# Value projection of four recurrent heads in 512-column matmuls, and a shared ring of three, in a hybrid decoder layer

## The chip, the cores and the metric

The kernel runs on one core of one Trainium2 chip. The metric is device time in microseconds, the median of several executions. Beside it stands one execution taken by the hardware profiler, whose span and rows are quoted below. The engines are TensorE (PE for its matmuls, PEld for its weight loads), VectorE (DVE), ScalarE (ACT), GpSimd (POOL) and SyncE (SP), which issues most of the transfers.

## The reference

One decoder layer over 2048 positions of width 1024, all in float32. The input is normalised and projected. Four recurrent heads (key and value width 128) and eight attention heads with a window of 128 read the projection; their outputs are joined, projected and added to the input. A gated feed-forward part with a causal convolution of width three and a last normalisation follow. Cut to the lines that matter here:

```python
u = rmsnorm(h, norm_mix_w[l])
proj = u @ w_in[l]
hq, hf, hi, hg, att = jnp.split(proj, [...], axis=-1)
f = lb + (1.0 - lb) * jax.nn.sigmoid(hf)
k_hg = 1.0 - f
v_hg = hi.reshape(B, S, HG_HEADS, HG_DV)          # four heads of 128 columns
o_hg = hgrn2_chunkwise(q_hg, k_hg, v_hg, log_f)   # S_t = diag(f_t) S_{t-1} + k_t v_t^T, o_t = S_t^T q_t
o_hg = rmsnorm(o_hg, hg_norm_w[l]) * silu(hg)
...
h = h + mix @ w_out[l]
```

The change touches `hi @ w`, the value projection, and the products that the recurrence needs.

## The kernel before

The sequence is worked through in two halves of 1024 positions. Each half has a mixing part (attention and recurrent heads, then the output projection) and a feed-forward part. Activations lie transposed, channels on partitions.

**Precision.** Every large product is made of three matmuls in a reduced float32 format. An operand is split into `hi`, its rounded copy, and `lo`, the rest: `hi*hi + hi*lo + lo*hi`. For weights `prep` does it (lines L192 on ACT and L193 on DVE), from a raw tile that SyncE fetches into a ring of three ("raw", L184). The two results go into a ring of two ("hi", "lo"), or, with `slots`, into the eight slots with the tag "m" that also hold queries, gates and later results.

**A unit** (`unit`, L214) projects to 128 channels: eight contraction tiles, three matmuls each, for two banks of 512 positions, so 48 matmuls with 512 moving columns.

**The value projection** (`project_v`, L706 to L710) is the one that puts positions on partitions. The stationary operand is a 128x128 tile of the input, the moving one the weights. Before, it serves two heads at a time: for each of eight position tiles 24 matmuls with 256 moving columns, and then two ACT instructions (L710) that scale each head's 128 columns into the head's own tile. It is called in heads 0 and 2 of each half, after the query unit of the attention.

**A recurrent head** (`hgrn`) goes through stages, each ended by a `yield`: the units f and hq; then element products whose sums over channels are made on PE (`summed_products`: d on DVE, L546, hi on ACT, L547, lo on DVE, L548, two matmuls into `pdiag`, L550 and L551); then levels of 1, 2, 4, 8, 16, 32 and 64 positions. For each level beyond the first, ACT gathers parts of QK into a tile G (L598), PE multiplies them (`plev`, L604 and L609), and DVE multiplies QK by the decay (L612) and places the results into ST. Then come transposes (`pkn`), the state updates (`pu` and SS, L657), the gate unit g, the outputs (`po`, L671 and L672), a normalisation and last transposes (`pot`, L687). Banks of PSUM for `pdiag`, `plev`, `pkn`, `pu`, `po` and `pot` come from a pool of two.

**An attention pair** (`attend`) makes its query unit, scores (`psc`), softmax, transposes (`ppt`) and outputs (`poT`).

**Order.** The main loop steps the two generators alternately. A planner turns this order into one fixed queue per engine: an earlier instruction in the program has precedence, but a later one may overtake it when the earlier isn't ready. So PE runs units of the next head while a chain waits. In heads 0 and 2 the query unit and the value projection stand as follows, and head 3 makes its gate unit ahead of the levels:

```python
elif h % 2 == 0:
    next(at)
    wv = [prep(a["w_v"][h // 2, s]) for s in range(2)]
    next(hg)
    vs += project_v(hf, wv, X, rs, p)
else:
    next(hg)
    next(at)
```

The output projection (`out_proj`, matmuls `pop`) can start only when all units of the half are done, since its operands take over the input's tiles; its third unit is held behind marks of head 3 (`BEHIND`).

Of the kernel before, what the change touches and what calls it, by code (L numbers as in the profile page):

```python
# [8 lines left out]
F32 = mybir.dt.float32  # L9
F32R = mybir.dt.float32r  # L10
U32 = mybir.dt.uint32
I32 = mybir.dt.int32
AF = mybir.ActivationFunctionType
# [4 lines left out]
P = 128  # L18
D = 1024
KT = D // P  # L20
# [3 lines left out]
TT = HALF // P  # L24
NB = HALF // 512
HG = 4
# [13 lines left out]
NEG = -1.0e30  # L40
UT = 7
RAW = 3
VB = 2
GB = 2
WARM = 12
TAIL_WARM = 7
LV = 4
# [3 lines left out]
def hymba_layer(ctx: ExitStack, tc: tile.TileContext, a: dict, out: bass.AP):  # L51
    nc = tc.nc

    def pool(name, bufs=1, space=None, stack=ctx, **kw):
        if space is not None:
            kw["space"] = space
        return stack.enter_context(tc.tile_pool(name=name, bufs=bufs, **kw))
# [12 lines left out]
    def ps(kind, name):  # L70
        return spaces[kind].tile([P, 512], F32, tag=kind, name=name)
# [109 lines left out]
    def raw4(src):  # L181
        t = wp.tile([P, D], F32, tag="raw", name="raw", bufs=RAW)
        if src is not None:
            nc.sync.dma_start(t, src)  # L184
        return t

    def prep(src, slots=False):

        raw = raw4(src)
        hi, lo = [hp.tile([P, D], F32R, tag="m", name=f"w{t}", bufs=KT) if slots else  # L190
                  wp.tile([P, D], F32R, tag=t, name=f"w{t}", bufs=2) for t in ("hi", "lo")]
        nc.scalar.copy(hi, raw)  # L192
        nc.vector.tensor_tensor(lo, raw, hi.bitcast(F32), op=ALU.subtract)  # L193
        return hi, lo
# [327 lines left out]
    def hgrn(hf, h, X, invb, vs, WG, mix, p, fu=None):  # L522
# [18 lines left out]
        ST = p.tile([P, TT, P], F32, tag="t4", name="ST", bufs=2)  # L541
        def summed_products(x, y):

            d = p.tile([P, 512], F32, tag="dd", name="dd", bufs=2)
            hi, lo = [p.tile([P, 512], F32R, tag="dg", name=n, bufs=4) for n in ("dh", "dl")]
            nc.vector.tensor_tensor(d, x, y, op=ALU.mult)  # L546
            nc.scalar.copy(hi, d)  # L547
            nc.vector.tensor_tensor(lo, d, hi.bitcast(F32), op=ALU.subtract)  # L548
            o = ps("hg", "pdiag")
            nc.tensor.matmul(o, ones_r, hi, start=True, stop=False)  # L550
            marks[1] = nc.tensor.matmul(o, ones_r, lo, start=False, stop=True)  # L551
            return o
# [35 lines left out]
        for m in LEVELS:  # L588
# [7 lines left out]
            if m > 1:  # L596
                G = p.tile([P, 2, HALF // 2], F32, tag="G", name="G", bufs=GB)
                nc.scalar.copy(G.rearrange("p t (b c m) -> p t b c m", c=2, m=m), far)  # L598
                pl = ps("hg", "plev")
                if m == 32:  # L600
                    for c in range(TT):
                        for b in range(2):
                            x = slice(c % R * P + b * 64 + c // R * m, c % R * P + b * 64 + c // R * m + m)
                            nc.tensor.matmul(pl[2 * b * m:2 * b * m + m, c * m:(c + 1) * m], G[:, 1, x], G[:, 0, x],  # L604
                                             start=True, stop=True)
# [33 lines left out]
        v = vs[h]  # L639

        Kn = p.tile([P, TT, P], F32, tag="t4", name="Kn", bufs=2)
        for b in range(NB):
            pk = ps("hg", "pkn")
            for i in range(4):
                c = slice((b * 4 + i) * P, (b * 4 + i + 1) * P)
# [3 lines left out]
        for b in range(NB):  # L649
            pu = ps("hg", "pu")  # L650
            for i in range(4):
                c = 4 * b + i
                marks["pu"] = nc.tensor.matmul(pu[:, i * P:(i + 1) * P], Kn[:, c], v[:, c], start=True, stop=True)
            for i in range(4):
                c = 4 * b + i
# [11 lines left out]
        for c in range(TT):  # L667
            cs = slice(c * P, (c + 1) * P)
            prev = state[:, h] if c == 0 else SS[:, c - 1]
            o = po[c // 4][:, c % 4 * P:(c % 4 + 1) * P]  # L670
# [5 lines left out]
        rs = rsqrt(ss, TT, 1.0 / P)  # L676
# [7 lines left out]
        for b, bs in halves():  # L684
# [4 lines left out]
            if h == HG - 1:  # L689
                hi, lo = mix[h]  # L690
# [4 lines left out]

    def project_v(hf, parts, X, rs, p):

        v = [p.tile([P, TT, P], F32, tag="v", name="v", bufs=VB) for _ in range(2)]
        for tt in range(TT):
            o = ps("mm", "pvv")  # L700
            t = slice(tt * P, (tt + 1) * P)
            for kt in range(KT):
                hi, lo = parts[kt // 4]
                xh, xl = X[kt]
                c = slice((kt % 4) * 256, (kt % 4 + 1) * 256)
                nc.tensor.matmul(o[:, 0:256], xh[:, t], hi[:, c], start=kt == 0, stop=False)  # L706
                nc.tensor.matmul(o[:, 0:256], xl[:, t], hi[:, c], start=False, stop=False)
                nc.tensor.matmul(o[:, 0:256], xh[:, t], lo[:, c], start=False, stop=kt == KT - 1)
            for i in range(2):
                nc.scalar.activation(v[i][:, tt], o[:, i * P:(i + 1) * P], AF.Identity, scale=rs[:, tt:tt + 1])  # L710
        return v

    def split_into(h, l, src, eng=None):
        return (nc.scalar.copy(h, src),  # L714
# [480 lines left out]
    for hf in range(NH):  # L1195
        X, kv, invb, rs, f0 = nxt
        with ExitStack() as st:
            p = pool(f"mix{hf}", stack=st, reuse_waits="tile")
            KS, V = att_keys(hf, kv, invb, p)
            mix = [None] * KT  # L1200
            vs = []
            M, WG = {}, {}
            for h in range(HG):
                hg = hgrn(hf, h, X, invb, vs, WG, mix, p, f0 if h == 0 else None)
                at = attend(hf, h, X, invb, KS, V, mix, p)
                with tc.issue_after(summed.ins) if hf + h == 0 else ExitStack():
                    next(hg)
                if h == HG - 1:
                    next(at)
                    next(hg)  # L1210
                    for kt in (0, 4, 1, 5, 2, 6):
                        M[kt] = split(mix[kt])
                    next(hg)
                elif h % 2 == 0:
                    next(at)
                    wv = [prep(a["w_v"][h // 2, s]) for s in range(2)]
                    next(hg)
                    vs += project_v(hf, wv, X, rs, p)
                else:
                    next(hg)  # L1220
                    next(at)
                if h < HG - 1:
                    WG[h] = prep(a["w_g"][h])
                next(at)
                next(hg)
                if h < HG - 1:
                    next(hg)
                next(at)
                if h < HG - 1:
# [5 lines that stand above are left out]
            M[7], M[3] = mix[7], mix[3]  # L1235
        with ExitStack() as st:
            p = pool(f"ffn{hf}", stack=st, reuse_waits="tile")
            kept, ops, hs, first, last = out_proj(hf, M, p)
            acts = gate_up(hf, ops, hs, first, last, p)
            nxt = down(hf, kept, acts, p)  # L1240


def _layout(i):

    import numpy as np

    def cols(w, idx):
        t = w[:, idx].reshape(KT, P, len(idx))
        return t.transpose(1, 0, 2).reshape(P, -1)

    x = i["x"][0]
    w_in = i["w_in"][0]
    ar = np.arange
    att0 = 2048
    att = [np.concatenate([att0 + j * HD + ar(HD), att0 + (j + 4) * HD + ar(HD)]) for j in range(4)]
    att += [att0 + 512 + ar(P), att0 + 640 + ar(P)]
    b = i["b_attn"][0]
    rows = [ar(P) + h * P for h in range(4)]
    rows += [512 + np.concatenate([j * HD + ar(HD), (j + 4) * HD + ar(HD)]) for j in range(4)]
    w_out = i["w_out"][0][np.concatenate(rows)]  # L1260
    w_v = np.stack([cols(w_in, 1024 + pr * 256 + ar(256)).reshape(P, 2, D).transpose(1, 0, 2) for pr in range(2)])
    conv = np.concatenate([i["conv_w"][0], i["conv_b"]], 0)
    d = {
        "xT": x.T.reshape(KT, P, S),
        "norm_mix_w": i["norm_mix_w"][0].reshape(KT, P).T,
        "w_q": np.stack([cols(w_in, h * P + ar(P)) for h in range(4)]),
        "w_f": np.stack([cols(w_in, 512 + h * P + ar(P)) for h in range(4)]),
        "w_v": w_v,
        "w_g": np.stack([cols(w_in, 1536 + h * P + ar(P)) for h in range(4)]),
        "w_att": np.stack([cols(w_in, c) for c in att]),  # L1270
        "b_attn": np.stack([b[c - att0] for c in att], 1),
        "lb_logits": i["lb_logits"].reshape(2, HG, P).transpose(2, 0, 1),
        "hg_norm_w": i["hg_norm_w"].reshape(P, 1),
        "sinks": i["sinks"].reshape(2, 4).T.reshape(1, 8),
        "w_out": np.stack([cols(w_out, t * P + ar(P)) for t in range(KT)]),
        "norm_ffn_w": i["norm_ffn_w"].reshape(KT, P).T,
        "final_norm_w": i["final_norm_w"].reshape(KT, P).T,
        "w_gate": np.stack([cols(i["w_gate"][0], t * P + ar(P)) for t in range(FT)]),
        "w_up": np.stack([cols(i["w_up"][0], t * P + ar(P)) for t in range(FT)]),
        "conv": conv.reshape(4, FT, P).transpose(2, 1, 0),  # L1280
    }

    w = i["w_down"][0].reshape(FT // 2, 2, P, 2, 4, P)
    d["w_down"] = w.transpose(3, 1, 2, 0, 4, 5).reshape(4, P, FT // 2, 512)
    return {k: np.ascontiguousarray(v) for k, v in d.items()}
# [16 lines left out]
```

## Time and profile before

| | |
|---|---|
| median of three executions | 2175.64 us (2173.93 to 2177.19) |
| the profiled execution | 2174.83 us, its span 2173.1 us |
| mean granted TensorE clock | 0.999 |
| PE / PEld busy | 99% / 83% of the span |
| DVE / ACT busy | 76% / 50% |
| mean share of the DMA engines | 119 GB/s moved |

Busy time is the union of the instructions' intervals. Matmuls are pipelined and overlap, so PE's busy share says that it is never idle for long, not that each matmul needs its duration. Rows of instruction groups give line, engine, operation, what it writes and reads, partitions and elements, count, and then busy us, mean ns of one, and the idle time before. Rows of the timeline give start and duration in us.

### The profile page before, as it was taken

The page shows a single profiled execution, that of the slowest core. Times are in us where ns is not written, and L with a number is a line of the kernel's source. Part 1 is how long each engine was busy: PE and PEld are TensorE (multiplying, and loading weights), DVE is VectorE, ACT ScalarE, POOL GpSimd, SP SyncE. Part 2 cuts the span into 40 slices and gives each one's busy share as a digit, 9 for nine tenths or more (in the row PEclk, how much of TensorE's full clock was granted, in tenths as well). Part 3 has the DMA queues.
Part 4 walks back from the last instruction along what each step waited for, and adds up shares of the span by engine and source line. Part 5 has one row for each costly group of instructions (what it writes and reads, how often), then busy time and mean ns, then how long its engine had stood idle before and what let it go on. Part 6 is the DMA issues. An engine that isn't in the chain of part 4 may idle for free.

```text
span 2173.1 us, 29038 instructions
## 1 busy us (share of the span) xinstructions
PE 2151.3 (99%) x11136; PEld 1809.6 (83%) x11136; DVE 1659.9 (76%) x2446; ACT 1094.1 (50%) x1902; POOL 6.0 (0%) x28
## 2 busy tenths in 40 slices
PE   9999999999999999999999999999999999999998
PEld 7988987888888888788889889878888888888888
DVE  6677677688887878785866776777978888887766
ACT  6556556564444445335736466555544443444353
POOL 1000000000000000000000000000000000000000
PEclk9999999999999999999999999999999999999999
DMA  4101112413232235964631111124133323259643
GB/s 156 49 30 39 49 40 78 136 59 127 92 126 89 96 117 167 375 223 163 205 127 39 42 37 49 47 70 147 58 116 102 117 82 126 93 190 396 226 142 131
DMA packets 94387, 258.09 MB, mean 119 GB/s; under 512 B 11416, under 2 KB 17576, under 8 KB 94248
## 3 DMA queue, kind: packets, MB, share of 16 engines
q1 hardware_dynamic: 88992, 251.30, 34.2%
q10 hardware_dynamic: 5256, 4.94, 0.8%
q8 instruction: 87, 1.43, 0.3%
q14 instruction: 52, 0.43, 0.1%
HBM read 195.10 MB, written 57.15 MB: 116 GB/s over the span
## 4 chain that ended last, share of the span: by engine, by line
PE 93%; DVE 3%; ACT 2%; DMA 1%; issue 1%; SPq 0%; ACTq 0%; DVEq 0%
PE X L885 7%; PE pop L214 7%; PE X L887 7%; PE X L886 7%; PE hq L214 4%; PE f L214 4%; PE q L214 4%; PE g L214 4%; PE Y L885 4%; PE Y L886 4%; PE Y L887 4%; PE pdx L1098 3%; PE pdx L1096 3%; PE pdx L1097 3%; PE pdy L1096 3%; PE pdy L1097 3%
## 5 line engine op out<-in xcount | busy, mean ns | idle before, releaser
L714 ACT CAST whi<-raw 128x1024 fp32r<-128x1024 f32 x88 | 92.6, 1052 | 109.1 <-PE X L886 68.2
L885 PE MATMUL X<-T,whi 128*128 128x512 f32 x352 | 136.9, 389 | 0.0
L886 PE MATMUL X<-T,whi 128*128 128x512 f32 x352 | 136.9, 389 | 0.0
L887 PE MATMUL X<-T,wlo 128*128 128x512 f32 x352 | 136.9, 389 | 0.0
L980 DVE SCALAR_TENSOR_TENSOR y<-ga,cw,y 128x1024 f32<-128x1024 f32 x88 | 112.4, 1280 | 26.0 <-ACT y L978 26.0
L892 ACT COPY u<-X 128x512 f32<-128x512 f32 x88 | 51.5, 585 | 133.2 <-PE X L887 133.0
L715 DVE TENSOR_TENSOR wlo<-raw,whi 128x1024 fp32r<-128x1024 f32 x88 | 107.2, 1219 | 0.0
L715 DVE TENSOR_TENSOR xld<-raw,xhd 128x1024 fp32r<-128x1024 f32 x72 | 80.9, 1132 | 21.7 <-ACT xhd L714 21.2
L192 ACT CAST whi<-raw 128x1024 fp32r<-128x1024 f32 x57 | 59.9, 1050 | 72.2 <-PE pop L214 28.6
L714 ACT CAST xhd<-raw 128x1024 fp32r<-128x1024 f32 x72 | 69.6, 977 | 47.3 <-DMA raw<-act1T 15.5
L193 DVE TENSOR_TENSOR wlo<-raw,whi 128x1024 fp32r<-128x1024 f32 x57 | 69.2, 1217 | 26.4 <-ACT whi L192 26.3
L214 PE MATMUL pop<-XH,wlo 128*128 128x512 f32 x256 | 85.9, 390 | 0.0
L214 PE MATMUL pop<-XL,whi 128*128 128x512 f32 x256 | 85.2, 390 | 0.0
L214 PE MATMUL pop<-XH,whi 128*128 128x512 f32 x256 | 85.0, 393 | 0.0
L886 PEld LDWEIGHTS X<-T,whi 128*128 128x128 f32 x352 | 66.1, 188 | 13.8
L885 PEld LDWEIGHTS X<-T,whi 128*128 128x128 f32 x352 | 66.1, 188 | 13.7
L887 PEld LDWEIGHTS X<-T,wlo 128*128 128x128 f32 x352 | 66.1, 188 | 13.7
L1096 PE MATMUL pdx<-xhd,hid 128*128 128x512 f32 x192 | 74.5, 392 | 1.9 <-ACT hid L714 1.0
L1097 PE MATMUL pdx<-xld,hid 128*128 128x512 f32 x192 | 74.8, 390 | 0.0
L612 DVE TENSOR_TENSOR QK<-QK,f 128x1024 f32<-128x1024 f32 x56 | 68.5, 1223 | 8.2 <-ACT G L598 7.6
L1098 PE MATMUL pdx<-xhd,lod 128*128 128x512 f32 x192 | 73.7, 389 | 0.0
L706 PE MATMUL pvv<-whi,XH 128*128 128x256 f32 x256 | 72.7, 286 | 0.0
(384 smaller groups left out, 6601.1 us busy)
## 6 DMA issues: line engine op xcount, KB each, us to landing
wr<-in_w_down SPq DMA_DIRECT2D x90, 512.0 KB, 5.5
raw<-in_w_gate SPq DMA_DIRECT2D x44, 512.0 KB, 3.7
raw<-in_w_up SPq DMA_DIRECT2D x44, 512.0 KB, 3.7
raw<-act0T SPq DMA_DIRECT2D x20, 512.0 KB, 3.9
raw<-act1T SPq DMA_DIRECT2D x20, 512.0 KB, 5.7
act0B<-y SPq DMA_DIRECT2D x33, 256.0 KB, 2.2
act1B<-y SPq DMA_DIRECT2D x33, 256.0 KB, 2.8
raw<-in_w_out SPq DMA_DIRECT2D x16, 512.0 KB, 6.2
```

The source lines that it names most:

```text
L193: nc.vector.tensor_tensor(lo, raw, hi.bitcast(F32), op=ALU.subtract)
L214: marks["unit"] = nc.tensor.matmul(o[b], w, x[:, bs], start=f, stop=l)
L706: nc.tensor.matmul(o[:, 0:256], xh[:, t], hi[:, c], start=kt == 0, stop=False)
L714: return (nc.scalar.copy(h, src), (eng or nc.vector).tensor_tensor(l, src, h.bitcast(F32), op=ALU.subtract))
L715: (eng or nc.vector).tensor_tensor(l, src, h.bitcast(F32), op=ALU.subtract))
L885: nc.tensor.matmul(o, wh[:, ws], xh, start=i == 0 and not more, stop=False, skip_group_check=more)
L886: nc.tensor.matmul(o, wh[:, ws], xl, start=False, stop=False, skip_group_check=more)
L887: r = nc.tensor.matmul(o, wl[:, ws], xh, start=False, stop=i == 3, skip_group_check=more)
L980: nc.vector.scalar_tensor_tensor(y, g[:, w:w + HALF], C.cw[:, ft, w:w + 1], y, op0=ALU.mult, op1=ALU.add)
L1096: nc.tensor.matmul(o, wh[:, i, c], ah[:, i, cols], start=f, stop=False, skip_group_check=more)
L1097: nc.tensor.matmul(o, wh[:, i, c], al[:, i, cols], start=False, stop=False, skip_group_check=more)
L1098: nc.tensor.matmul(o, wl[:, i, c], ah[:, i, cols], start=False, stop=l, skip_group_check=more)
```

## The change

`project_v` is called once in each half, in head 0, for all four heads: its matmuls have 512 moving columns, one ACT instruction evacuates all four heads of a position tile, and the values lie in one tile for four heads. The value weights are laid out in four tiles of two contraction tiles each; the first two are split into the ring of two, the last two into "m" slots. Head 2 now takes the same order of steps as head 1. In `summed_products` the tiles "dd" (two of 512) and "dg" (four of 512) are gone; d takes one slot and the pair hi, lo another slot of the ring "G" of the gathered copies, whose slots hold 2 x 512 and whose number goes from two to three.

```diff
-VB = 2
-GB = 2
+GB = 3
...
-            d = p.tile([P, 512], F32, tag="dd", name="dd", bufs=2)
-            hi, lo = [p.tile([P, 512], F32R, tag="dg", name=n, bufs=4) for n in ("dh", "dl")]
+            d = p.tile([P, 2, 512], F32, tag="G", name="dd", bufs=GB)[:, 0]
+            both = p.tile([P, 2, 512], F32R, tag="G", name="dh", bufs=GB)
+            hi, lo = both[:, 0], both[:, 1]
...
     def project_v(hf, parts, X, rs, p):
 
-        v = [p.tile([P, TT, P], F32, tag="v", name="v", bufs=VB) for _ in range(2)]
+        v = p.tile([P, HG, TT, P], F32, name="v")
         for tt in range(TT):
             o = ps("mm", "pvv")
             t = slice(tt * P, (tt + 1) * P)
             for kt in range(KT):
-                hi, lo = parts[kt // 4]
+                hi, lo = parts[kt // 2]
                 xh, xl = X[kt]
-                c = slice((kt % 4) * 256, (kt % 4 + 1) * 256)
-                nc.tensor.matmul(o[:, 0:256], xh[:, t], hi[:, c], start=kt == 0, stop=False)
-                nc.tensor.matmul(o[:, 0:256], xl[:, t], hi[:, c], start=False, stop=False)
-                nc.tensor.matmul(o[:, 0:256], xh[:, t], lo[:, c], start=False, stop=kt == KT - 1)
-            for i in range(2):
-                nc.scalar.activation(v[i][:, tt], o[:, i * P:(i + 1) * P], AF.Identity, scale=rs[:, tt:tt + 1])
-        return v
+                c = slice((kt % 2) * 512, (kt % 2 + 1) * 512)
+                nc.tensor.matmul(o, xh[:, t], hi[:, c], start=kt == 0, stop=False)
+                nc.tensor.matmul(o, xl[:, t], hi[:, c], start=False, stop=False)
+                nc.tensor.matmul(o, xh[:, t], lo[:, c], start=False, stop=kt == KT - 1)
+            nc.scalar.activation(v[:, :, tt], o.rearrange("p (h d) -> p h d", h=HG), AF.Identity,
+                                 scale=rs[:, tt:tt + 1])
+        return [v[:, h] for h in range(HG)]
...
-                elif h % 2 == 0:
+                elif h == 0:
                     next(at)
-                    wv = [prep(a["w_v"][h // 2, s]) for s in range(2)]
+                    wv = [prep(a["w_v"][s], s > 1) for s in range(4)]
                     next(hg)
                     vs += project_v(hf, wv, X, rs, p)
...
-    w_v = np.stack([cols(w_in, 1024 + pr * 256 + ar(256)).reshape(P, 2, D).transpose(1, 0, 2) for pr in range(2)])
+    w_v = cols(w_in, 1024 + ar(512)).reshape(P, 4, D).transpose(1, 0, 2)
```

The tiles take the same room: per partition 8 KB for two value tiles, 8 KB for G, 4 KB for dd and 8 KB for dg before; 16 KB and 12 KB after.

## The prediction

> **What bounds the kernel now.** I read the page's first part, then the waits of TensorE (PE), then the busy time by stage of the first half of the sequence.
>
> ```profile
> span 2173.1 us, 29038 instructions
> PE 2151.3 (99%) x11136; PEld 1809.6 (83%) x11136; DVE 1659.9 (76%) x2446; ACT 1094.1 (50%) x1902; POOL 6.0 (0%) x28
> ...
> PE poT L508 <- DVE pp L500: 3.5, 5, 1.5
> PE pu L653 <- ACT Kn L647: 2.5, 2, 1.4
> ```
>
> PE is the bound, nearly everywhere; its largest waits (us in total, times, longest) come where the last recurrent head of a half ends. Columns of the next view: stretch and length, then busy us and instructions of PE, PEld, DVE, ACT, POOL, then clock and DMA.
>
> ```profile
> 69.11:97.80 28.69, 28.69 (x267) 28.41 (x266) 16.39 (x27) 18.33 (x37) 0.00 (x0) 1.00 0.12 37
> ...
> 155.20:234.40 79.20, 79.20 (x517) 68.21 (x516) 64.85 (x119) 51.53 (x115) 0.00 (x0) 1.00 0.14 40
> ...
> 307.90:352.77 44.87, 44.87 (x259) 38.07 (x258) 42.98 (x63) 31.28 (x48) 0.00 (x0) 1.00 0.39 117
> ...
> 353.00:380.00 27.00, 23.32 (x185) 19.80 (x184) 17.32 (x46) 13.01 (x58) 0.00 (x0) 1.00 0.01 2
> 1430.90:1457.90 27.00, 23.42 (x186) 19.79 (x185) 17.03 (x44) 13.07 (x58) 0.00 (x0) 1.00 0.01 2
> ```
>
> The five stretches are: value projection of head 0; head 1; head 3 up to the end of its levels; the rest of head 3; and that same rest in the second half. PE is full in the first three. DVE is idle 12.3 us beside the projection (28.69 - 16.39), but takes 82% of head 1 (64.85 of 79.20) and 96% of head 3's first stretch (42.98 of 44.87). In the rest of head 3 PE idles 3.7 us (27.00 - 23.32), 3.6 us in the second half: there the chain of head 3 is late and PE has nothing else. So PE work removed is worth its full time only while the recurrent chains keep up with the shorter queue.
>
> **The matmuls.** The duration of a matmul is not its price, because they overlap; the distance of starts is. First and last row of 11 projection matmuls in a row, and of 12 with 512 moving columns that also change their weights each time:
>
> ```profile
> 78.33 0.28 PE L706 MATMUL pvv<-whi,XH 128*128 128x256 f32 x1
> ...
> 79.53 0.28 PE L707 MATMUL pvv<-whi,XL 128*128 128x256 f32 x1
> ...
> 504.10 0.39 PE L885 MATMUL X<-T,whi 128*128 128x512 f32 x1
> ...
> 506.60 0.39 PE L887 MATMUL X<-T,wlo 128*128 128x512 f32 x1
> ```
>
> 256 columns: 1.20 / 10 = 0.120 us. 512 columns: 2.50 / 11 = 0.227 us. Each of three lines (L706 to L708) runs 256 times, 768 in all; they become 384 of double width. 768 x 0.120 = 92.2 us; 384 x 0.227 = 87.3 us. The change takes **4.9 us** of PE work away, 2.4 us per half. (Durations would say 768 x 0.286 - 384 x 0.389 = 70 us, which is wrong.)
>
> ```profile
> L885 PE MATMUL X<-T,whi 128*128 128x512 f32 x352 | 136.9, 389 | 0.0
> ...
> L706 PE MATMUL pvv<-whi,XH 128*128 128x256 f32 x256 | 72.7, 286 | 0.0
> ```
>
> [...]
>
> **Evacuation.** 64 ACT instructions of 128x128 become 16 of 128x512, for which a scaled copy of that size gives the price:
>
> ```profile
> L710 ACT ACTIVATE v<-pvv,y 128x128 f32<-128x128 f32 x64 | 20.1, 362 | 12.4 <-PE pvv L708 12.4
> ...
> L784 ACT ACTIVATE h<-h,nfw 128x512 f32<-128x512 f32 x28 | 19.2, 719 | 16.8 <-DMA keep<-h 16.8
> ```
>
> 64 x 0.362 = 23.2 us against 16 x 0.719 = 11.5 us. ACT is 50% busy, and in head 3, where it could matter, nothing changes on it: worth nothing, covered by PE's own work.
>
> **Weights.** The splits are as many as before (L192 on ACT, L193 on DVE), but four now stand ahead of the first projection instead of two.
>
> ```profile
> L193 DVE TENSOR_TENSOR wlo<-raw,whi 128x1024 fp32r<-128x1024 f32 x57 | 69.2, 1217 | 26.4 <-ACT whi L192 26.3
> ...
> L192 ACT CAST whi<-raw 128x1024 fp32r<-128x1024 f32 x57 | 59.9, 1050 | 72.2 <-PE pop L214 28.6 <-PE hq L214 13.6 <-PE q L214 8.4
> ```
>
> Two more are 2 x (1.05 + 1.22) = 4.5 us at most, and go into slots of "m" that don't wait for the unit ring. In the first half SyncE's queue fetched the value weights long before the projection's start at 69.11; in the second the slots come free when the last outputs have left, and the projection starts at 1146:
>
> ```profile
> 26.43 5.54 SPq L184 DMA_DIRECT2D raw<-in_w_v  x2
> 33.00 0.33 SPq L184 DMA_DIRECT2D raw<-in_w_g  x1
> ...
> 1106.44 4.69 SPq L1191 DMA_DIRECT2D out<-h  x8
> 1111.24 3.41 SPq L184 DMA_DIRECT2D raw<-in_w_v  x2
> 1125.20 0.33 SPq L184 DMA_DIRECT2D raw<-in_w_g  x1
> ...
> 1146.47 0.28 PE L706 MATMUL pvv<-whi,XH 128*128 128x256 f32 x1
> ```
>
> The gate weights, issued at 33.00, queue behind two more fetches, and are needed only after the projection. I take nothing; the bound is 4.5 us a half if the cover were gone. In head 2 the two splits vanish from a busy DVE, but others take their turn.
>
> **The ring of three.** A product's tile d, and the pair hi/lo, each take a slot that the gathers G also use. The gather of level 2 now has to wait until one of the first two pairs has been read by its `pdiag` matmuls. Before, it ran ahead of them: in head 3 DVE was at the second level's product while the first `pdiag` (quoted below) was still ahead.
>
> ```profile
> 313.31 0.69 DVE L546 TENSOR_TENSOR dd<-QK 128x512 f32<-128x512 f32 x1
> ...
> 316.99 1.23 DVE L612 TENSOR_TENSOR QK<-QK,f 128x1024 f32<-128x1024 f32 x1 [0.53 <-ACT G L598]
> 318.25 0.63 DVE L619 TENSOR_TENSOR f<-f 128x256 f32<-128x256 f32 x1
> ...
> L598 ACT COPY G<-QK x48: 1035/1052/1189, 65.1 to 1425.7; 128x1024 f32<-128x1024 f32 x48
> ```
>
> The wait stands before ACT's gather; behind it DVE's product waits, since the gather reads what it overwrites. 1.9 us of DVE work (1.23 + 0.63) moves behind 318.82, and if level 1's d is held too, all from 313.31 to 318.88, 5.6 us. That is the loss bound per half, in head 3 alone; in head 0 the longer projection covers it. The other side: with three slots a later gather waits for the level three back, not two, which could gain as much as one gather, 1.05 us by the last row, on each of the last three levels, 3.2 us a half. The ends lie about zero and I take zero.
>
> **The chain against the queue.** This is the term that decides. Head 1 has no projection in its body, and head 2 will be like it. Landmarks on PE (first `pdiag` of heads 1, 2 and 3; first and last gathered level of heads 2 and 3; last transpose of head 3):
>
> ```profile
> 155.24 0.40 PE L550 MATMUL pdiag<-dh,ones_r 128*128 128x512 f32 x1
> ...
> 226.82 0.28 PE L706 MATMUL pvv<-whi,XH 128*128 128x256 f32 x1
> ...
> 234.40 0.39 PE L550 MATMUL pdiag<-dh,ones_r 128*128 128x512 f32 x1
> ...
> 239.59 0.27 PE L609 MATMUL plev<-G 128*128 128x128 f32 x1
> ...
> 252.35 0.39 PE L609 MATMUL plev<-G 128*128 128x128 f32 x2
> ...
> 318.82 0.40 PE L550 MATMUL pdiag<-dh,ones_r 128*128 128x512 f32 x1
> ...
> 331.13 0.27 PE L609 MATMUL plev<-G 128*128 128x128 f32 x1
> ...
> 349.97 0.38 PE L609 MATMUL plev<-G 128*128 128x128 f32 x2
> ...
> 379.10 0.27 PE L687 MATMUL pot<-ident,on 128*128 128x128 f32 x1
> ```
>
> Head 1's chain took 234.40 - 155.24 = 79.2 us, and in its last 7.6 us PE was already on head 2's projection. Before, head 2's lasted 84.4 us, filled by that projection. I keep the clock of this trace and leave out what head 0 gains in length. Up to about 380 PE has 380 - 3.7 idle - 192 x 0.120 (head 2's projection) = 353.3 us of work. The chain ends at 234.40 + P + tail: P is head 2's time, tail is head 3 from its first `pdiag` to the end.
>
> P lies between 67.6 us (head 1's 64.85 us of DVE at the 96% that head 3 shows) and 79.2 us (head 1 again). I take 76, nearer to the row that is the same program, less something because PE's queue is shorter. The tail before was 61.2 us, but 12.3 of it waited for the gate unit; without that it is 5.2 (239.59 - 234.40) + 48.9 (380 - 331.13) = 54.1, and with levels as fast as head 2's (12.8 against 18.8 us, since the splits for the output projection will be out of the way) 48.1. I take 48.1. Idle time is then 234.4 + 76 + 48.1 - 353.3 = 5.2 us instead of 3.7: 1.5 us a half given back.
>
> **The sum.** -4.9 + 2 x 1.5 = -1.9 us. The profiled execution took 2174.83 us (span 2173.1, 1.7 around it) and would take 2172.9. The median, 2175.64, is 0.8 above that execution: forecast **2173.7 us**, no change that can be told. What a measurement can tell is 0.2%, 4.35 us, so 2171.3 to 2180.0.
>
> **The rivals.**
>
> *The saving arrives and the tail closes.* For it: DVE's 96% where inputs wait. P = 72 with the short tail gives an idle time of 1.2 us, so (1.2 - 3.7 - 2.4) x 2 = -9.8: 2165.8. With no idle time left it is (0 - 3.7 - 2.4) x 2 = -12.2, 2163.4, the floor. Against: head 1 ran at 82% of DVE without any idle PE to blame. It decides below P of about 74.7, where the result passes 2171.3.
>
> *Head 3's chain becomes the bound: slower.* For it: head 1 is the only head without a projection, and it took 79.2. The projection's 23 us then cover head 0, where DVE had nothing to do anyway, and are missing in head 3, which starts with too little queued behind it; only two units of the output projection, 72 matmuls or 16.4 us, may run before it. P = 79.2 with the short tail: idle 8.4, (8.4 - 3.7 - 2.4) x 2 = +4.6, 2180.2; with the long tail 14.4 and +16.6, 2192.2. Against: PE's queue is shorter, so the chain's own matmuls get in sooner. It decides above P of about 79 with the short tail, or 73 with the long one.
>
> *The wide matmul doesn't run at 0.227 us*, so that nothing is saved: against it the 512-column rows, with new weights at each matmul. It has no weight of its own.
>
> **How the numbers follow.** Chances: forecast 0.37, faster rival 0.35, slower rival 0.28, each with its side of the 4.35 us. The forecast's own range is 2171.3 to 2180.0. Eight times in ten: from 2163.5, the floor, to 2186, half way from the short to the long tail at P = 79.2 (2180.2 + 12.0 / 2 = 2186.2), which leaves out the rest.
>
> **What would show it.** Matmuls of line `project_v` 0.227 us apart, 384 of them, and none in head 2. A first `pdiag` of head 2 about 20 us later than before (its projection in head 0 is 43.6 us instead of 23.0), and head 3's first `pdiag` 76 us after that. PE's idle time in the rest of head 3 near 5 us; DVE above 85% from head 2 on. I am wrong if head 2 takes under 74 or over 79 us, if PE waits for value weights at the start of the projection, or if ACT's gathers of level 2 hold up head 3.

## The result, and the profile after

| | before | changed kernel |
|---|---|---|
| median, 14 runs each on one chip | 2175.72 us (2171.36 to 2177.67) | 2170.23 us (2168.80 to 2173.02) |
| ratio, 95% interval | | 0.9978 (0.9970 to 0.9986) |
| the profiled execution, its span | 2174.83, 2173.1 us | 2170.70, 2169.0 us |

The forecast was 2173.7 us, 1.9 less than before. The changed kernel is 5.5 us faster here (interval 3.0 to 6.5), and 3.3 us (2.2 to 5.9) on a second chip, where both ran again: faster, at the bound of what can be told, inside the 80% range and 1.1 us below the forecast's own range. That is the side of the faster rival, which had a chance of 0.35 against the forecast's 0.37; taken with the second chip's difference, 3.3 us, the result would lie inside the forecast's range.

The first part of the changed kernel's page: span, and PE's busy time and instructions (384 matmuls fewer).

```profile
span 2169.0 us, 28228 instructions
PE 2150.5 (99%) x10752; PEld 1792.4 (83%) x10752; DVE 1659.2 (76%) x2446; ACT 1091.9 (50%) x1858; POOL 6.0 (0%) x28
```

Where the 4.1 us of the two spans lie is read from busy time by stretch. I cut each execution at its first attention query of a half and at the first `X` matmul behind the output projection's first units: mixing, the rest of the first half, mixing, the rest of the second. The kernel before:

```profile
57.29:445.50 388.21, 384.53 (x2442) 332.56 (x2440) 283.07 (x509) 223.80 (x513) 0.00 (x0) 1.00 0.20 62
445.50:1134.65 689.15, 686.50 (x3034) 565.57 (x3032) 544.14 (x700) 320.41 (x431) 0.00 (x0) 1.00 0.45 152
1134.65:1523.78 389.13, 385.55 (x2457) 333.51 (x2456) 282.19 (x503) 224.45 (x513) 0.00 (x0) 1.00 0.19 62
1523.78:2173.10 649.32, 640.97 (x2965) 534.56 (x2963) 513.09 (x676) 291.21 (x406) 0.00 (x0) 1.00 0.44 149
```

The changed kernel:

```profile
57.25:444.54 387.29, 384.20 (x2249) 324.39 (x2248) 282.80 (x509) 222.93 (x491) 0.00 (x0) 1.00 0.20 62
444.54:1130.99 686.45, 684.84 (x3033) 564.44 (x3032) 543.77 (x700) 320.21 (x431) 0.00 (x0) 1.00 0.44 153
1130.99:1520.51 389.52, 386.56 (x2265) 324.87 (x2264) 282.42 (x503) 223.01 (x491) 0.00 (x0) 1.00 0.20 62
1520.51:2169.00 648.49, 640.35 (x2965) 534.49 (x2963) 512.85 (x676) 291.52 (x406) 0.00 (x0) 1.00 0.43 149
```

The surprise: the two mixing stretches, the only ones that the change touches, differ by -0.92 and +0.39 us, where the forecast had about -1.0 for each, and -2.70 and -0.83 come from stretches with the same work. Part of that is the granted clock. It is 0.50 for 3.4 us at a time, in these windows, first of before, then of the changed kernel:

```profile
1096.40:1099.80 3.40, 3.40 (x10) 2.63 (x9) 3.30 (x15) 1.04 (x1) 0.00 (x0) 0.50 0.10 34
```

```profile
357.30:360.70 3.40, 3.32 (x16) 3.27 (x16) 3.40 (x7) 1.55 (x4) 0.00 (x0) 0.50 0.00 0
1432.50:1435.90 3.40, 3.25 (x16) 2.96 (x15) 3.40 (x7) 1.46 (x4) 0.00 (x0) 0.50 0.11 32
```

Each can cost PE up to 1.7 us, half of 3.4 at a clock of 0.50, an estimate. Leaving out one behind the last matmul of each execution, before has one, in the second stretch; the changed kernel has two, one in the rest of head 3 of each half. So a span's 4.1 us can't be read as the change alone; the experiments below go by medians.

The rows that the prediction asked for, from the changed kernel's timeline of PE: projection matmuls 0.227 us apart (2.49 / 11), the first `pdiag` of heads 1, 2 and 3, the first gathered level of head 3 and its last transposes (eight, in one row).

```profile
78.38 0.39 PE L706 MATMUL pvv<-whi,XH 128*128 128x512 f32 x1
...
80.87 0.39 PE L707 MATMUL pvv<-whi,XL 128*128 128x512 f32 x1
...
175.86 0.40 PE L550 MATMUL pdiag<-dh,ones_r 128*128 128x512 f32 x1
...
253.07 0.40 PE L550 MATMUL pdiag<-dh,ones_r 128*128 128x512 f32 x1
...
325.99 0.40 PE L550 MATMUL pdiag<-dh,ones_r 128*128 128x512 f32 x1
...
334.71 0.49 PE L609 MATMUL plev<-G 128*128 128x128 f32 x3
...
378.15 1.03 PE L687 MATMUL pot<-ident,on 128*128 128x128 f32 x8
```

P is 325.99 - 253.07 = 72.9 us, and the tail 52.9 us, up to the start of the last of the eight transposes (378.15 + 1.03 - 0.27 = 378.9). The stretches of head 0's projection, of P, of head 3's levels and of the rest of head 3 in both halves:

```profile
69.00:112.70 43.70, 43.70 (x242) 36.68 (x242) 20.45 (x30) 20.23 (x31) 0.00 (x0) 1.00 0.16 48
...
253.07:325.99 72.92, 72.47 (x462) 61.69 (x461) 60.54 (x112) 48.74 (x110) 0.00 (x0) 1.00 0.13 41
325.99:353.00 27.01, 27.01 (x179) 23.28 (x178) 24.83 (x42) 21.94 (x42) 0.00 (x0) 1.00 0.47 151
353.00:379.00 26.00, 23.36 (x178) 19.85 (x176) 19.03 (x48) 12.08 (x51) 0.00 (x0) 0.93 0.02 5
1429.00:1455.00 26.00, 23.18 (x179) 19.61 (x178) 18.23 (x49) 11.91 (x54) 0.00 (x0) 0.93 0.02 6
```

PE idles 2.6 and 2.8 us in the rest of head 3 (26.00 - 23.36, 26.00 - 23.18) where the forecast had 5.2, and 3.7 and 3.6 were idle before.

### The profile page after: what moved, and what is told of

Its sections match the earlier page's. It is cut to its first block, busy times and chain, and to the rows that moved or that the text cites. A ratio compares the mean times of both kernels' runs of the same rounds, so it can differ in the third digit from the quotient of the medians.

```text
span 2169.0 us, 28228 instructions
## 1 busy us (share of the span) xinstructions
PE 2150.5 (99%) x10752; PEld 1792.4 (83%) x10752; DVE 1659.2 (76%) x2446; ACT 1091.9 (50%) x1858; POOL 6.0 (0%) x28
## 4 chain that ended last, share of the span: by engine, by line
PE 92%; ACT 2%; DVE 2%; DMA 2%; issue 1%; ACTq 0%; SPq 0%; DVEq 0%
PE X L885 7%; PE X L886 7%; PE X L887 7%; PE pop L213 7%; PE q L213 4%; PE hq L213 4%; PE g L213 4%; PE Y L887 4%; PE Y L886 4%; PE Y L885 4%; PE pdx L1096 3%; PE f L213 3%; PE pdx L1098 3%; PE pdx L1097 3%; PE pdy L1096 2%; PE pdy L1098 2%
## 5 line engine op out<-in xcount | busy, mean ns | idle before, releaser
L1097 PE MATMUL pdx<-xld,hid 128*128 128x512 f32 x192 | 74.7, 389 | 0.0
L885 PE MATMUL X<-T,Sh 128*128 128x512 f32 x176 | 68.7, 390 | 1.5 <-ACT s L892 1.5
```

The source lines that it names most:

```text
L885: nc.tensor.matmul(o, wh[:, ws], xh, start=i == 0 and not more, stop=False, skip_group_check=more)
L1097: nc.tensor.matmul(o, wh[:, i, c], al[:, i, cols], start=False, stop=False, skip_group_check=more)
```

## The experiments

Four kernels ran together on each of three chips, each beside 27 runs of the kernel before. Differences are against that median on the same chip (2173.74, 2174.18 and 2175.05 us).

| place of the projection | columns | ring | median us | difference | ratio, 95% |
|---|---|---|---|---|---|
| heads 0 and 2 | 256 | three | 2184.36 | +10.6 | 1.0048 (1.0035 to 1.0060) |
| heads 0 and 2 | 256 | five | 2173.88 | -0.3 | 0.9999 (0.9990 to 1.0007) |
| head 0 | 256 | three | 2176.86 | +3.1 | 1.0015 (1.0006 to 1.0024) |
| head 0 | 256 | five* | 2176.10 | +1.0 | 1.0008 (0.9999 to 1.0017) |
| head 0 | 512 | three | 2170.41 | -3.3 | 0.9982 (0.9973 to 0.9990) |
| head 0 | 512 | three* | 2170.92 | -4.1 | 0.9978 (0.9970 to 0.9987) |
| head 0 | 512 | five* | 2171.88 | -3.2 | 0.9986 (0.9977 to 0.9995) |

\* keeps the values of heads 0 and 1 only, as told below.

**The ring alone.** To the kernel before, only the lines of `summed_products` and the ring's number:

```diff
-GB = 2
+GB = 3
...
+            d = p.tile([P, 2, 512], F32, tag="G", name="dd", bufs=GB)[:, 0]
+            both = p.tile([P, 2, 512], F32R, tag="G", name="dh", bufs=GB)
```

> The kernel before with the ring of three alone: products and gathered copies share three slots, the value projection stays in heads 0 and 2 with 256 columns. Theory (the gain is the width of the matmuls, the ring is worth nothing): within 2 us of before. Rival (the ring lets the late levels run ahead, and that is the gain): 3 us or more faster. Third (the gather of level 2 waits for the first products' matmuls in head 3): up to 1.9 us a half slower, 4 us in all.

2184.36 us: the part that I had priced at zero costs 10.6 us. The third theory had the sign, but at most 4 us. What it does is seen on PE's waits (total, times, longest), and then on ACT's and PE's timeline in head 3:

```profile
PE pkn L647 <- ACT ST L637: 7.6, 2, 3.8
```

```profile
357.86 1.28 ACT L485 ACT_TABLE_LOAD   x1
...
359.27 0.39 ACT L483 ACTIVATE sc<-sc,m 128x128 f32<-128x128 f32 x1
...
362.47 0.75 ACT L637 COPY ST<-plev 64x256 f32<-64x256 f32 x2
```

```profile
363.27 1.11 PE L647 MATMUL pkn<-ident,QK 128*128 128x128 f32 x4 [3.79 <-ACT ST L637]
```

The delay isn't paid where it arises, at the gather of level 2, but 40 us later: the last level is late enough that ACT starts the attention's exponentials (L483) ahead of copying that level out (L637), the bank isn't free, and PE stands 3.8 us in each half. Before, ACT copied it out ahead of the first exponential:

```profile
352.82 0.37 ACT L636 COPY ST<-plev 64x256 f32<-64x256 f32 x1
...
354.62 0.39 ACT L483 ACTIVATE sc<-sc,m 128x128 f32<-128x128 f32 x1
```

In the first half the clock was at 0.50 from 362.6 on, 0.7 us before that wait ended, for 6.8 us, and in the second for 3.4 us:

```profile
362.60:369.40 6.80, 6.08 (x27) 5.68 (x28) 4.40 (x10) 2.33 (x6) 0.00 (x0) 0.50 0.01 2
1444.70:1448.10 3.40, 3.26 (x15) 2.86 (x15) 2.90 (x6) 1.46 (x4) 0.00 (x0) 0.50 0.00 0
```

The loss lies in the two mixing stretches:

```profile
58.87:452.65 393.78, 387.87 (x2441) 335.47 (x2440) 283.51 (x509) 223.29 (x513) 0.00 (x0) 0.99 0.20 61
...
1139.09:1533.10 394.01, 387.79 (x2457) 335.01 (x2456) 282.82 (x503) 224.59 (x513) 0.00 (x0) 1.00 0.19 61
```

They are 5.6 and 4.9 us longer than before. Of these 10.5 us PE is idle for 4.9 more and busy for 5.6 more with the same matmuls; half of the 10.2 us at a clock of 0.50, 5.1, an estimate, can account for most of the latter.

**The same with five slots.** The same edit with `GB = 5`, the room of the three separate tiles before.

> The kernel before, with d and the pair hi/lo in the ring of the gathers as in the change, but with five slots (20 KB a partition, the same room as the three separate tiles before). Theory A (the ring costs because with three slots the gather of level 2 waits for the first pdiag): with five slots that wait is gone, so no difference from before, -2 to +2 us. Rival B (sharing one ring at all couples the products with the gathers, whatever the number): still +5 to +11 us, as the ring of three alone.

2173.88 us, as before. It is the number of slots that costs, not that products and gathers share a ring.

**The width.** The changed kernel, each matmul as two of 256 columns in two banks:

```diff
-                nc.tensor.matmul(o, xh[:, t], hi[:, c], start=kt == 0, stop=False)
...
+                for i in range(2):
+                    c = slice((kt % 2) * 512 + i * 256, (kt % 2) * 512 + (i + 1) * 256)
+                    nc.tensor.matmul(os[i], xh[:, t], hi[:, c], start=kt == 0, stop=False)
...
+            for i, o in enumerate(os):
+                nc.scalar.activation(v[:, 2 * i:2 * i + 2, tt], o.rearrange("p (h d) -> p h d", h=2), AF.Identity,
```

> The changed kernel, but each 512-column matmul of the value projection as two of 256 columns into two banks: all four heads are still projected in head 0, and the ring is the changed one. Theory (the width is the gain): 4.9 us of PE work come back, so 3 to 5 us slower than the changed kernel and within 2 us of before. Rival (the place in head 0 or the ring is the gain): within 1.5 us of the changed kernel. Rival (the place costs, since head 3 has less queued): slower than before by 2 us or more.

Beside it ran the changed kernel once more:

> The changed kernel once more, on the chip of the others. All theories: 4 to 6 us faster than before. If its granted clock falls at the end of head 3 in both halves as in its first profile, PE's idle time there is what lets it fall; if not, that fall belongs to one execution.

2176.86 against 2170.41 us: the width, with the second bank and evacuation that go with it, is worth 6.4 us with three slots. The expectation was 3 to 5 us, and at most 2 above before, where 3.1 are measured. The changed kernel itself is 3.3 us faster than before on this chip, not the 4 to 6 expected. Its profile has the mean granted clock of the first, 0.998, and the same busy time of PE in the two mixing stretches (384.18 and 386.55 us, 384.20 and 386.56 in the first), where head 2's old order, at a clock of 1.000, has 382.86 and 385.21. That fits falls in both executions; their place in the second is not shown.

**Head 2's order.** The changed kernel with the attention's query ahead of the element products in head 2, as before:

```diff
+                elif h == 2:
+                    next(at)
+                    next(hg)
```

> The changed kernel with head 2's old order of steps, the attention's query unit ahead of the levels. Theory (head 2's chain is what sets head 3's start): its first products wait for the query unit, head 3's first pdiag comes later, and the kernel is 2 to 5 us slower than the changed one. Rival (PSUM banks and DVE set the chain, not the order): within 1 us of the changed kernel.

2171.16 us (ratio to before 0.9985, 0.9976 to 0.9994), 0.8 us from the changed kernel, inside the rival's 1 us: no difference.

**Five slots in the new place.** The values of four heads leave no room for them, so two kernels keep the values of heads 0 and 1 only, which heads 2 and 3 read as well (their recurrences are then of other values; all matmuls and products remain):

```diff
-        v = p.tile([P, HG, TT, P], F32, name="v")
+        v = p.tile([P, 2, TT, P], F32, name="v")
...
-        return [v[:, h] for h in range(HG)]
+        return [v[:, h % 2] for h in range(HG)]
```

> The changed kernel with the ring of five instead of three. For room it keeps only the values of heads 0 and 1 (half of each evacuation); heads 2 and 3 read those, so their recurrences are wrong; all matmuls stay. Theory A (the three slots cost in the changed kernel what they cost alone, 10.6 us): 5 to 10 us below the control with three slots, 2160-2166 us. Theory B (PE is full up to the end of head 3, and the three slots cost only where that makes PE idle, which the new place has closed): within 2 us of the control.

> Control for the ring of five: the changed kernel with three slots that keeps only the values of heads 0 and 1, read by heads 2 and 3 too. Both theories: as the changed kernel, 2 us either way, 2168.5-2172.5 us, since the evacuation lies beside PE's work.

2171.88 us with five slots against 2170.92 with three. In the changed kernel the short ring costs nothing, taken as a whole. The slots alone are not separated, since the order of the queues changes with them. The timelines of ACT (first row) and PE with five slots:

```profile
311.95 1.21 ACT L598 COPY G<-QK 128x1024 f32<-128x1024 f32 x1 [1.20 <-DVE t L176]
...
334.02 0.40 PE L550 MATMUL pdiag<-dh,ones_r 128*128 128x512 f32 x1
...
355.80 0.52 PE L460 MATMUL psc<-KS,qh 128*128 128x256 f32 x1 [3.26 <-DVE sc L469]
...
378.41 1.03 PE L687 MATMUL pot<-ident,on 128*128 128x128 f32 x8
```

The gather of level 2 runs 17.4 us earlier than in the changed kernel (311.95 against 329.37), head 3's first `pdiag` comes 8.0 us later (334.02 against 325.99), and the last transposes come at the same time (378.41 against 378.15). PE waits 3.3 us for the scores' banks in each half, where three slots have 0.4 in the first; such waits can hide what the longer ring gives the chain.

**The place alone.** With 256 columns, five slots, and values left out in the same way (both evacuations go to the two heads kept):

> The place alone: all four heads' value projection in head 0, but in matmuls of 256 columns, with the ring of five; values of heads 2 and 3 left out as in the control. Theory A (the place gains 7.5 us whatever the ring): 7 us below the kernel before, 2165-2168 us. Theory B (the place only takes back what the three slots lose): -2 to +2 us against the kernel before. Width: 5 to 7 us above the same with 512 columns.

2176.10 us: +1.0 us, as theory B had it, and 4.2 us above the 512 columns with five slots, less than the 5 to 7 expected. The place as such gains nothing. It takes back 7.5 us (10.6 to 3.1) of what the three slots lose. At 256 columns the two rings differ by 2.1 us in the new place, on two chips and with intervals that overlap, so it isn't shown that the short ring is free there.

**Banks and slots.** The two diagonal products take their `pdiag` banks from the attention's pool, and in head 3 come ahead of the scores; in a second kernel d goes to the attention's ring instead (banks as changed, same order); a third has both:

```diff
-            o = ps("hg", "pdiag")
+            o = ps(kind, "pdiag")
...
-            pd = summed_products(q[:, bs], K[:, bs])
+            pd = summed_products(q[:, bs], K[:, bs], "at")
...
-            d = p.tile([P, 2, 512], F32, tag="G", name="dd", bufs=GB)[:, 0]
+            d = p.tile([P, 512], F32, tag="pp", name="dd", bufs=4)
...
         if h == HG - 1:
+            yield
             gate()
...
                 if h == HG - 1:
+                    next(hg)
                     next(at)
                     next(hg)
```

> The changed kernel; the two diagonal products take their pdiag banks from the attention's pool ('at') and not from the head's own ('hg'), and in head 3 they stand ahead of the attention's scores in the program. Ring and matmul width as changed. Theory A (in head 3 the ring only hands on the lateness of the first pdiag, which waits for a bank until head 2's last transposes are read at 322 us): first pdiag of head 3 at about 312-316 instead of 326 us, gather of level 2 right behind, last transpose of head 3 some 5 us earlier, PE idle in the rest of head 3 (2.6 + 2.8 us) mostly gone: 4 to 8 us below the changed kernel, 2163-2167 us. Rival B (PE's queue is full anyway, the chain has cover): within 2 us of the changed kernel.

> The changed kernel; d takes a slot of the attention's ring of four ('pp') and no longer one of the shared ring, so that a product takes one of the three slots and not two; in head 3 the products stand ahead of the scores in the program. Banks as changed. Theory A (the first pdiag is late because of its bank, and the gather of level 2 waits for it whatever the slots): the gather of level 2 still stands behind the first pdiag, within 2 us of the changed kernel. Rival C (the number of slots that the products take is the price): level 1's d and the first gather run ahead, 4 to 8 us below the changed kernel.

> Both edits together: pdiag banks from the attention's pool, and d in the attention's ring. Theory A: as with the banks alone, 4 to 8 us below the changed kernel, at most 2 us more from the slots. Rival C: as with the slots alone. If both waits stand one behind the other, only this one gains. Rival B (PE full): all three within 2 us of the changed kernel.

2175.02, 2182.08 and 2178.58 us: 0.8, 7.9 and 4.4 us slower than before (the first within noise, ratio 0.9998 to 1.0016), and so all slower than the changed kernel, which is 3.3 to 5.5 us faster than before; no theory had that. The banks did what they were to do, and it bought nothing. From the timeline of PE of the kernel with the banks alone:

```profile
307.68 0.50 PE L550 MATMUL pdiag<-dh,ones_r 128*128 128x512 f32 x1
...
378.29 1.03 PE L688 MATMUL pot<-ident,on 128*128 128x128 f32 x8
```

The first `pdiag` of head 3 is 18.3 us earlier than in the changed kernel, the last transposes 0.1 us later. It has waits that weren't there; its row for the next half's first unit, against 0.4 in the changed kernel, is the largest:

```profile
PE kv L213 <- DVE y L177: 2.5, 1, 2.5
```

Why d in the attention's ring is 7.1 us slower still than the banks I have not taken apart.

**Filling the idle time.** 16 matmuls without use behind the level of 16 of head 3, in a bank of the attention:

```diff
+        if h == HG - 1:
+            without_use(ps("at", "idle"), 16, marks[16])
```

> The changed kernel with 16 matmuls of 128 columns without use behind the level of 16 in head 3 of each half, which only fill PE where it waits. Clock theory (the granted clock falls to 0.5 for 3.4 us behind short waits of PE at 354 and 1430 us, and that costs 1.7 us a half): no fall in head 3, 2 to 3.4 us below the changed kernel, 2167-2168.5 us. Rival (PE's queue is late by as much work as is put in, or the fall costs nothing because the chain waits elsewhere): 0 to +4 us, 2170.4-2174 us.

2191.42 us (1.0078, 1.0065 to 1.0090), far worse than either expectation: the attention's transposes moved behind the recurrent outputs, and PE stood still for them for 4.08 us, with the clock at 0.50 for 10.2 us from 368.8 on, within that wait. From the timeline of PE, and the stretch at half clock:

```profile
370.56 1.94 PE L496 MATMUL ppt<-ident,sc 128*128 128x128 f32 x8 [4.08 <-DVE sc L487]
```

```profile
368.80:379.00 10.20, 7.51 (x45) 6.57 (x46) 9.21 (x28) 5.06 (x27) 0.00 (x0) 0.50 0.01 2
```

So it says nothing on what the clock alone costs. That the attention's banks have no slack in head 3 is how I read it; no run tests it alone.

## Why the prediction was right or wrong

**The matmuls** (4.9 us): right, and the heart of the gain. Two pairs of kernels that differ in width give 6.4 and 4.2 us, on either side of it. The distance of starts was right (0.227 us, 2.49 / 11).

**Evacuation and weights** (nothing): no run contradicts it. The evacuation takes 11.0 us, 0.5 less than priced, and PE never waits for value weights: these are all PE's waits between 60 and 450 us, and no wait of the second half is at a value matmul either.

```profile
L709 ACT ACTIVATE v<-pvv,y 128x512 f32<-128x512 f32 x16 | 11.0, 688 | 35.9 <-PE pvv L708 35.9
```

```profile
PE plev L609 <- ACT G L598: 1.2, 1, 1.2
PE ppt L496 <- DVE sc L469: 1.0, 1, 1.0
PE psc L460 <- DVE sc L469: 0.4, 1, 0.4
PE poT L507 <- DVE po L499: 0.2, 1, 0.2
PE poT L507 <- DVE pp L499: 0.2, 1, 0.2
```

**The ring of three** (zero): right for the whole change, wrong as a price of this edit. The loss bound, 5.6 us a half, is near what it costs alone (10.6 / 2 = 5.3) by luck: the bound was DVE's delayed work, and what PE loses there is a wait of 3.8 us for ACT, which takes the softmax first, and the time at a clock of 0.50 that goes with it. I had named "ACT's gathers of level 2 hold up head 3" as a sign of being wrong. They do stand behind `pdiag` in the changed kernel (gather at 329.37, below), with no loss of time.

```profile
329.37 1.20 ACT L598 COPY G<-QK 128x1024 f32<-128x1024 f32 x1
```

**The chain against the queue** (1.5 us a half given back): this is the step that failed. Its end was right by luck, by errors that cancel. Taking off the 20.6 us by which head 0 became longer (175.86 - 155.24), head 2's first `pdiag` was 1.9 us earlier than I had kept it, P 3.1 us shorter than 76 (at 72.9 it is below 74, which I had named as a sign of being wrong), the tail 4.8 us longer than 48.1: the chain ends at 378.9 - 20.6 = 358.3 where the forecast had 358.5. But I took the whole distance between that end and PE's work as idle time. In the rest of head 3 PE idles 2.6 us, not 5.2, since it had 2 us more to get through up to there; up to 1.7 of these, by the estimate above, are the clock of 0.50 from 357.30 on. DVE was busy 83% of head 2 (60.54 of 72.92), 92% of the levels (24.83 of 27.01) and 73% of the rest (19.03 of 26.00), where I had named more than 85% from head 2 on. What sets the end is not shown. The place alone was to cost 3.0 us in all and costs 1.0; its interval, -0.2 to 3.7, still holds 3.0, so it is the idle time in the trace that shows the step wrong.

**The rivals.** *The saving arrives and the tail closes* had the right sign and P (72.9, below its 74.7), not its mechanism: the tail did not close to 48.1. *Head 3's chain becomes the bound: slower* is refuted by the time, and an earlier start of that chain didn't help: with its first `pdiag` 18.3 us earlier, or with its first gather 17.4 us earlier, the end of head 3 stayed where it was. In the old place, by contrast, head 3 had no such slack, and there the short ring cost 10.6 us. What gives it the slack in the new place is argued, not shown: I read it as the 23 us of projection that no longer stand between head 2's chain and head 3's.

**What stays open.** 2.7 us of the profiled 4.1 lie in the stretch from 444.54 to 1130.99, where the change has no work. That stretch is 686.44 us with the ring alone too, whose total is 10.6 us worse, so it is not the projection's doing. It goes with PE's busy time: of twelve profiled executions, each of another kernel or of the changed one again, six took 687.2 to 689.9 us there, with PE busy for 686.0 to 686.5, and six 685.5 to 687.1, with 684.3 to 684.9 and the same work (3033 or 3034 matmuls in each trace). Before is one of the first six, with 1.7 us more than the changed kernel (686.50 against 684.84); its clock was at 0.50 for 3.4 us there, which accounts for up to 1.7 us, an estimate, and the changed kernel's didn't fall there. The order of DVE and ACT around the second half's first norm differs from kernel to kernel as well, and no run separates what is left.

## What to carry to other kernels

Price each part of a change for the place where it will stand: the short ring cost 10.6 us in the old order and nothing that shows in the new one, and only runs of each part in both places showed it. Where PE is full, an earlier start of a chain can move nothing, as it did here by 18.3 us; ask first what else the end waits for. A wait that delays a chain may be paid far behind it, where an engine with two users (here ACT, between copying a level out and the softmax) takes them in another order.

## What the runs showed of the hardware

In head 3 the granted clock fell to 0.50 beside waits of PE of 0.99 to 4.08 us: for 3.4 us in each half of the changed kernel, for 6.8 and 3.4 us with the ring alone, for 10.2 us in the first half with the fill. In the first half of the changed kernel two waits, of 1.21 and 0.99 us, ended at 355.23 and 357.38, and the clock was at 0.50 from 357.3 on:

```profile
355.23 1.16 PE L609 MATMUL plev<-G 128*128 128x128 f32 x8 [1.21 <-ACT G L598]
...
357.38 1.97 PE L496 MATMUL ppt<-ident,sc 128*128 128x128 f32 x8 [0.99 <-DVE sc L469]
```

The kernel with head 2's old order has the same two waits 0.7 us later, and its clock stayed at 1.00:

```profile
355.93 1.16 PE L609 MATMUL plev<-G 128*128 128x128 f32 x8 [1.21 <-ACT G L598]
...
358.07 1.09 PE L496 MATMUL ppt<-ident,sc 128*128 128x128 f32 x8 [0.98 <-DVE sc L469]
```

```profile
357.30:360.70 3.40, 2.19 (x16) 1.71 (x16) 3.40 (x7) 1.78 (x6) 0.00 (x0) 1.00 0.00 0
```

The eight transposes take 1.97 us in one and 1.09 in the other. The same waits, with and without a fall, so their length doesn't decide alone: no wait in the changed kernel's head 3 of the first half is over 1.21 us, and the clock fell, while before had waits of 1.36 and 1.52 us in its rest of head 3 and was at 1.00 there. In the 3.4 us just ahead of its two falls (353.9 to 357.3, 1429.1 to 1432.5) the changed kernel's PE was busy 1.28 and 1.37 us. What decides is not shown.

Before's fall at 1096.4 has no such wait beside it: PE has none in the 10 us ahead of it. 16 matmuls of a single column (`pst`) took 1.84 us from 1093.78 on; the changed kernel has the same 16, also 1.84 us, from 1091.74 on and no fall there, so the cause of that one stays open too.

The clock also goes with part of the spread from run to run. The 27 runs of before beside the ring alone, by their mean granted clock: 2172.07 us at 1.000 (2 runs), 2173.44 at 0.999 (10), 2174.57 at 0.998 (11), 2175.89 at 0.997 (4), some 1.3 us for each thousandth. On this chip the mean clock goes with about a third of the variance of the 27 runs, on the two other chips with half and three quarters. At 0.998 the changed kernel took 2170.75 us (9 runs of the second measurement), 3.8 less than before; the ring alone, compared at 0.997 (one run), 7.7 us more. By that one run about 3 of its 10.6 us (10.6 - 7.7) would be the clock; its profile leaves room for up to 5.1, both estimates.
